# The first two value projections of a decoder block as seven block products, and the convolution's layer norm by token halves

## The chip, the cores and the metric

The kernel runs on one core of a Trainium2 chip. A core has a matrix engine (PE, whose weight loads the profile lists apart as PEld), a vector engine (DVE), a scalar engine (ACT), a general engine (POOL) and a queue that issues transfers (SP). Each engine runs its own instructions in a fixed order, and semaphores hold an instruction until what it needs is there. The metric is the device time of one execution in microseconds; the kernel before takes 1676.24 us in the median of three runs (1675.69 to 1677.17).

## The reference

One layer of a decoder block for 1024 tokens of 1024 channels, all float32. What matters here:

```
h  = rms_norm(x)
z  = h @ w_in            # q, k, v (3 groups x 8 heads x 64 each), conv input, two gates
o_g = attention of head group g on q, k, v     (g = 0, 1, 2; dilations 1, 4, 16)
u  = causal depthwise conv (31 taps) of a gated linear unit of z
m  = mean over the 1024 channels of u, per token
u  = silu((u - m) * rsqrt(mean((u - m)^2) + 1e-5) * g + b)     # layer norm, then swish
y  = u @ w_conv_out + b_conv_out
x  = x + rms_norm((sigmoid(z_ga) * y_attn + sigmoid(z_gc) * y) @ w_mix_out)
x  = x + rms_norm(swiglu_ffn(rms_norm(x)))
```

The value projection is `v = h @ w_v`, 1024 x 1024 times 1024 x 1536. The kernel cuts its columns into six jobs of 256: head group g (0, 1, 2) by half hg of its heads (0, 1).

## The kernel before, in words

**Number format.** Every float32 product is made of three products of rounded parts: a matrix is split into `hi` (a copy rounded to the matrix engine's format, by ACT) and `lo` (what is left, a subtraction by DVE or POOL), and hi*hi, hi*lo and lo*hi are added up in PSUM.

**Stages.** The convolution's inputs, the gates, and the 12 query and key pairs (`qk_pair`) come first. Each of these takes two jobs at once by `winograd`: the two jobs' weights by two halves of the contraction make a 2 x 2 block matrix A, the tokens by halves another one B, and seven block products of sums of blocks (A11, A12, A22, S1 to S4 with B11, B21, B22, T1 to T4) take the place of eight. The token operands, sums of halves already split, lie in SBUF as `B.T`. Then come the six value jobs, each by `v`, with the plain eight block products; then one gate, the convolution's output projection, the attention's, the mix and the FFN.

**What sets the order.** It is written out by hand. `tick()` is called after every few matmuls; it runs the steps that were put down for that tick (`later(n, step)`, in n ticks), splits one piece of the next weights every PIECE ticks, and moves every generator in `B.gens` on by one step; a generator that yields n rests n ticks. `beat()` is called more often and moves one generator, `B.fine`, at a rate: this is the attention, whose matmuls are so strewn between those of the value jobs. A tile that is taken from a pool of fixed size waits until the last reader of the tile that lay there is done.

**The value jobs** (`v`, L1114 to L1165). A job takes 8 token tiles by 8 contraction tiles. For each, one matmul (L1139) multiplies the tokens' hi by a weight tile that holds hi and lo side by side (512 columns), and one (L1140) the tokens' lo by hi (256 columns). ACT copies the 512 columns out (L1150), and POOL adds the two halves (L1161). The weights' split is L207 (ACT) and L208 (DVE). A tick falls after every two such pairs, 32 ticks a job.

**The convolution's norm** (`conv_norm`, L1488 to L1540) is a generator that runs beside the value jobs. It loads the eight channel blocks (128 channels by 1024 tokens), gets the mean by a product of the blocks' sum with a constant column (L1503; the sum is finished by a POOL addition, L893), subtracts it (DVE, L1512), squares (ACT, L1515), adds the squares up (DVE, L1518), and calls `rstd`: eight products of one column each (L469), a square root on ACT (L473), small steps on DVE, and eight transposes (L484) that spread the result over the partitions. Then it multiplies (DVE, L1530) and applies the swish (ACT, L1533). ACT changes its function table where the kind of function changes (ACT_TABLE_LOAD at L473, L1533 and L1538).

**The attention** (`attention`) starts when the norm's generator has ended (`normed` is 9). `double` (POOL, L1078 to L1080) lays out the keys of a head pair for two halves of the sequence: one operand z for each half, one part for each head. The scores are L1262 and L1266, the exponentials L1280, the transposes L1305 and the products with the values L1339.

## Time and profile before

| | |
|---|---|
| median of three runs | 1676.24 us |
| the profiled execution's own time | 1676.75 us |
| its span, first to last instruction | 1675.0 us |
| PE busy | 1658.9 us, 99% of the span |
| DVE, ACT, POOL busy | 1272.3, 828.3, 542.5 us |
| granted PE clock | 0.999 |
| value jobs' matmuls L1139 and L1140 | 384 of each, first at 544.2 us, last at 769.2 us |
| first attention matmul L1262 | 608.5 us |

A row of the timeline gives start, duration, engine, line, operation, tiles, partitions or columns of the weights, shape, and how many instructions were merged; brackets at its end hold the idle time before it and what ended that. A matmul's duration runs from its start until its result has drained, and matmuls overlap, so what one costs is the step from its start to the next one's. A row of a group gives its busy time, the mean of one in ns, and the idle time before it with what ended that.

### The profile page before, as it was taken

The page shows a single profiled execution, that of the slowest core. Times are in us where ns is not written, and L with a number is a line of the kernel's source. Part 1 is how long each engine was busy: PE and PEld are TensorE (multiplying, and loading weights), DVE is VectorE, ACT ScalarE, POOL GpSimd, SP SyncE. Part 2 cuts the span into 40 slices and gives each one's busy share as a digit, 9 for nine tenths or more (in the row PEclk, how much of TensorE's full clock was granted, in tenths as well). Part 3 has the DMA queues.
Part 4 walks back from the last instruction along what each step waited for, and adds up shares of the span by engine and source line. Part 5 has one row for each costly group of instructions (what it writes and reads, how often), then busy time and mean ns, then how long its engine had stood idle before and what let it go on. Part 6 is the DMA issues. An engine that isn't in the chain of part 4 may idle for free.

```text
span 1675.0 us, 23388 instructions
## 1 busy us (share of the span) xinstructions
PE 1658.9 (99%) x8027; PEld 1384.6 (83%) x8027; DVE 1272.3 (76%) x2268; ACT 828.3 (49%) x1646; POOL 542.5 (32%) x456
## 2 busy tenths in 40 slices
PE   9999999999999999999999999999999999999998
PEld 7787888888888889988788888888888888888886
DVE  7998987789899768778876746877655566576686
ACT  7454443443444588888713357633333333354453
POOL 0038777787876366877300300000000000000000
PEclk9999999999999999999999999999999999999999
DMA  4435433455566987879998524134232223494334
GB/s 182 153 102 187 143 132 126 153 176 192 177 176 161 286 273 224 257 220 286 297 272 310 176 88 171 56 132 151 84 118 94 95 95 119 165 375 120 115 119 157
DMA packets 165178, 289.64 MB, mean 173 GB/s; under 512 B 47689, under 2 KB 79812, under 8 KB 165060
## 3 DMA queue, kind: packets, MB, share of 16 engines
q1 hardware_dynamic: 164420, 287.45, 52.5%
q8 instruction: 63, 1.03, 0.3%
q14 instruction: 55, 0.45, 0.1%
q10 hardware_dynamic: 288, 0.52, 0.1%
q0 software_dynamic: 352, 0.18, 0.1%
HBM read 197.39 MB, written 95.42 MB: 175 GB/s over the span
## 4 chain that ended last, share of the span: by engine, by line
PE 87%; issue 5%; DVE 2%; POOL 2%; ACT 2%; DMA 1%; SPq 0%; DVEq 0%; ACTq 0%; POOLq 0%
PE p L354 16%; PE p L353 16%; PE p L352 16%; PE p L2282 13%; PE p L2026 5%; PE p L1139 5%; PE p L336 2%; PE p L337 2%; PE p L338 2%; PE p L1140 2%; PE p L655 2%; PE p L1339 2%; PE p L1305 1%; PE p L1266 1%; PE p L1262 1%
## 5 line engine op out<-in xcount | busy, mean ns | idle before, releaser
L352 PE MATMUL p<-b,b 128*128 128x512 f32 x1316 | 512.7, 390 | 0.1
L354 PE MATMUL p<-b,b 128*128 128x512 f32 x1316 | 512.4, 389 | 0.2
L353 PE MATMUL p<-b,b 128*128 128x512 f32 x1316 | 512.2, 389 | 0.1
L352 PEld LDWEIGHTS p<-b,b 128*128 128x128 f32 x1316 | 247.1, 188 | 52.7 <-ACT c L411 0.5
L354 PEld LDWEIGHTS p<-b,b 128*128 128x128 f32 x1316 | 247.1, 188 | 52.5 <-POOL b L215 1.5
L353 PEld LDWEIGHTS p<-b,b 128*128 128x128 f32 x1316 | 247.1, 188 | 51.7 <-DVE b L1477 0.5
L2282 PE MATMUL p<-b,b 128*128 128x512 f32 x924 | 209.6, 389 | 0.0
L2282 PEld LDWEIGHTS p<-b,b 128*128 128x128 f32 x924 | 173.5, 188 | 36.0
L868 DVE SCALAR_TENSOR_TENSOR p<-b,par,p 128x511 f32<-128x511 f32 (+14 forms) x232 | 163.6, 738 | 0.0
L1139 PE MATMUL p<-b,b 128*128 128x512 f32 x384 | 144.2, 408 | 0.1
L214 ACT CAST b<-d 128x1024 fp32r<-128x1024 f32 x82 | 86.1, 1050 | 100.7 <-POOL d L237 56.6
L215 POOL TENSOR_TENSOR b<-d,b 128x1024 fp32r<-128x1024 f32 x43 | 104.2, 2422 | 47.6 <-ACT b L214 39.0
L1477 DVE TENSOR_TENSOR b<-b,b 128x512 fp32r<-128x512 f32 x141 | 98.9, 708 | 16.0 <-ACT b L1476 14.4
L215 DVE TENSOR_TENSOR b<-d,b 128x1024 fp32r<-128x1024 f32 x39 | 47.6, 1221 | 79.3 <-ACT b L214 79.3
L1140 PE MATMUL p<-b,b 128*128 128x256 f32 x384 | 107.7, 280 | 0.0
L1476 ACT CAST b<-b 128x512 fp32r<-128x512 f32 x141 | 86.4, 619 | 40.9 <-PE p L2282 18.5
L336 PE MATMUL p<-b,b 128*128 128x512 f32 x240 | 96.3, 401 | 0.0
L214 ACT CAST b<-b 128x1024 fp32r<-128x1024 f32 x51 | 53.6, 1052 | 85.0 <-POOL b L246 38.7
L1280 ACT ACTIVATE c<-c,stat 128x128 f32<-128x128 f32 (+1 forms) x192 | 85.2, 447 | 18.2 <-DVE stat L1270 16.9
L337 PE MATMUL p<-b,b 128*128 128x512 f32 x240 | 93.6, 390 | 0.0
L338 PE MATMUL p<-b,b 128*128 128x512 f32 x240 | 93.6, 390 | 0.0
L2026 PE MATMUL p<-b,b 128*128 128x512 f32 x384 | 89.9, 392 | 0.0
(248 smaller groups left out, 2897.0 us busy)
## 6 DMA issues: line engine op xcount, KB each, us to landing
b<-w_in SPq DMA_DIRECT2D x33, 512.0 KB, 5.8
b<-w_fi SPq DMA_DIRECT2D x29, 512.0 KB, 4.4
d<-w_in SPq DMA_DIRECT2D x25, 512.0 KB, 4.2
dk<-c SPq DMA_DIRECT2D x48, 256.0 KB, 4.3
dq<-c SPq DMA_DIRECT2D x48, 256.0 KB, 3.6
b<-dk SPq DMA_DIRECT2D x48, 256.0 KB, 6.2
d<-w_fi SPq DMA_DIRECT2D x22, 512.0 KB, 3.5
dqS<-c SPq DMA_DIRECT2D x44, 256.0 KB, 2.1
```

What stands on the lines that cost most here:

```text
L214: self.nc.scalar.copy(hi, x)
L215: self.wsplit.tensor_tensor(lo, x, f(hi), op=OP.subtract)
L336: nc.tensor.matmul(ps, hi[:, s], a, start=kt == 0, stop=False)
L337: nc.tensor.matmul(ps, hi[:, s], b, start=False, stop=False)
L352: nc.tensor.matmul(ps, hi[:, s], a, start=first and kt == 0, stop=False, skip_group_check=True)
L353: nc.tensor.matmul(ps, hi[:, s], b, start=False, stop=False, skip_group_check=True)
L354: nc.tensor.matmul(ps, lo[:, s], a, start=False, stop=kt == 3, skip_group_check=True)
L868: nc.vector.scalar_tensor_tensor(A[i][:, j:], src[i][:, :H - j], w[i], A[i][:, j:], op0=OP.mult, op1=OP.add)
L1139: nc.tensor.matmul(ps, a, w, start=kt == 0, stop=kt == KT - 1, skip_group_check=True)
L1140: nc.tensor.matmul(ps[:, 256:], b, w[:, :256], start=False, stop=kt == KT - 1, skip_group_check=True)
L2026: nc.tensor.matmul(banks[tt][nh], st, wt[:, nh * H:(nh + 1) * H], start=bool(kt == 0 and a), stop=bool(kt == KT - 1 and b))
L2282: nc.tensor.matmul(acc[t], x, y, start=first and e == 0, stop=last and e == 2, skip_group_check=True)
```

## The change

Two of the six value jobs, (g, hg) = (0, 0) and (1, 0), are done together by a new function `quad` in the block form that the query and key pairs use, with seven products of 48 matmuls of 256 columns each. Here the tokens are the stationary side and the weights the moving side. The other four keep `v`. `quad` has its own loads, sums (DVE) and splits (cast on ACT, subtraction on POOL), written by ticks. Results leave PSUM by ACT copies and DVE additions.

`conv_norm` works by halves of the tokens (512 each): it takes its blocks half by half, and calls `rstd` twice, for 512 tokens each. The eight small products of the first half are issued while the squares of the second half run, those of the second half while the first half is multiplied and passed through the swish. It starts with the block products rather than with the first value job. The attention's first step (loads) and the laying out of all four parts of its first keys (`double`) are now put down by ticks before the first scores; the second half's parts were laid out at the head pair's second score step before.

```diff
+    def quad_split(self, q, name):
...
+        hi, lo = self.slot(F32R), self.slot(F32R)
+        nc.scalar.copy(hi, x)
...
+        nc.gpsimd.tensor_tensor(lo, x, f(hi), op=OP.subtract)
+        q["w"][name] = hi, lo
...
+    def quad_prod(self, ps, w, rhs, first):
+        nc = self.nc
+        hi, lo = w
+        for kt in range(4):
+            a, b = rhs[kt]
+            n = slice(kt * 256, (kt + 1) * 256)
+            for c in range(4):
+                o = ps[c // 2][:, c % 2 * 256:(c % 2 + 1) * 256]
+                t = slice(c * 128, (c + 1) * 128)
+                nc.tensor.matmul(o, a[:, t], hi[:, n], start=first and kt == 0 and c % 2 == 0, stop=False,
+                                 skip_group_check=True)
+                nc.tensor.matmul(o, a[:, t], lo[:, n], start=False, stop=False, skip_group_check=True)
+                nc.tensor.matmul(o, b[:, t], hi[:, n], start=False, stop=kt == 3 and c % 2 == 1, skip_group_check=True)
+                if c % 2:
+                    self.tick()
+
+    def quad(self, q, T, then):
...
+        ja, jb = q["jobs"]
+        for k, step in ((1, lambda: self.quad_split(q, "A12")), (5, lambda: self.quad_sum(q, "S4")),
+                        (9, lambda: self.quad_split(q, "S2")),
+                        (17, lambda: self.quad_split(q, "S1")), (25, lambda: self.quad_split(q, "S3")),
+                        (33, lambda: self.quad_split(q, "S4")), (41, lambda: self.quad_split(q, "A22"))):
+            self.later(k, step)
...
+        X, Z = two(), two()
+        self.quad_prod(X, w.pop("A11"), operands("B11"), True)
+        x1 = copy(X, ja, True)
+        self.quad_prod(Z, w.pop("A12"), operands("B21"), True)
+        add(Z, x1, ja, 0)
+        Z = x1 = None
+        self.quad_prod(X, w.pop("S2"), operands("T2"), False)
+        x2 = copy(X, ja)
+        V = two()
+        self.quad_prod(V, w.pop("S1"), operands("T1"), True)
+        v1 = copy(V, jb)
+        self.quad_prod(X, w.pop("S3"), operands("T3"), False)
+        add(X, v1, jb, 1)
+        v1 = None
+        self.quad_prod(V, w.pop("S4"), operands("B22"), False)
+        add(V, x2, ja, 1)
+        V = x2 = None
+        self.quad_prod(X, w.pop("A22"), operands("T4"), False)
+        o = result()
+        for b in range(2):
+            nc.scalar.activation(ordered(o[b], jb[0][0]), plain(X[b]), AF.Identity, scale=-1.0)
...
@@ attention @@
-        self.later(17, lambda p=nxt: self.double(p, 0))
+        for i in range(4):
+            self.later(17 + 2 * i, lambda p=nxt, i=i: self.double(p, i // 2, (i % 2,)))
...
-                if u == 1:
-                    self.double(cur, 1, (1,) if cur[2]["z"][1] else (0, 1))
+                if u == 1 and s:
+                    self.double(cur, 1, (1,))
...
@@ conv_norm @@
+        for j in range(4):
+            self.later((1, 3, 8, 11)[j], lambda j=j: load(0, j))
+        yield 5
+        means = [average(0), average(1)]
...
+        def total(hf):
+            scale[hf] = self.rstd(q[hf][0], H, self.eps_ln, 0)
+            next(scale[hf])
+            q[hf] = None
...
         for hf in range(2):
...
+            mean, means[hf] = means[hf], None
+            for b in range(10):
+                if b < 8:
+                    add(A[hf, b], A[hf, b], mean, op=OP.subtract)
+                if 0 < b < 9:
+                    q[hf].append(self.half())
+                    nc.scalar.activation(q[hf][-1], A[hf, b - 1], AF.Square)
...
+                if hf and b == 4:
+                    total(0)
+                if hf == 0 and b > 5:
+                    load(1, b - 6)
+                yield 1
+            mean = None
+        for hf in range(2):
+            rs = scaled(hf)
+            for b in range(9):
+                if hf == 0 and b == 4:
+                    total(1)
+                if b < 8:
+                    add(A[hf, b], A[hf, b], rs, op=OP.mult)
+                if b:
+                    a = A.pop((hf, b - 1))
+                    nc.scalar.activation(a, a, AF.Silu, bias=self.col(C_BLN + b - 1), scale=self.col(C_GLN + b - 1))
...
+                yield b % 2
...
@@ build @@
+    vs = list(vj.values()) + [late[:1] or co[:1]]
+    for i, q in enumerate(B.quads):
+        if i == QUADS - 1:
+            B.later(33, lambda: B.load_ahead(vs[0][0]))
+            B.later(43, lambda: next(att))
+            B.later(36, lambda: B.load_ahead(vs[0][1]))
+            B.later(41, lambda: B.queue_split(vs[0][1]))
+        B.quad(q, B.T, B.quads[i + 1] if i + 1 < QUADS else None)
+    B.T = None
+    B.banks(g=2, s=2, t=2, o=2)
```

In the rows below a matmul's names are its result, then its moving and its stationary operand. Line numbers of the kernel before are its own; in the changed kernel `quad_prod` is L1218 to L1221, the value jobs' pair is L1144 and L1145, L469 has become L474, and L207 has become L209.

**PE, where the value stage starts.** First the kernel before:

```order
L354 MATMUL p_4710<-b_1092,b_4770 128x512
L1139 MATMUL p_4880<-b_4800,b_631 128x512
L1140 MATMUL p_4880<-b_4800,b_631 128x256
L1139 MATMUL p_4880<-b_4800,b_642 128x512
L1140 MATMUL p_4880<-b_4800,b_642 128x256
L1139 MATMUL p_4880<-b_4820,b_652 128x512
L1140 MATMUL p_4880<-b_4820,b_652 128x256
```

and the changed one:

```order
L358 MATMUL p_4710<-b_1092,b_4774 128x512
L1218 MATMUL p_4872<-b_4818,b_631 128x256
L1220 MATMUL p_4872<-b_4819,b_631 128x256
L1221 MATMUL p_4872<-b_4818,b_631 128x256
L1218 MATMUL p_4872<-b_4818,b_631 128x256
L1220 MATMUL p_4872<-b_4819,b_631 128x256
L1221 MATMUL p_4872<-b_4818,b_631 128x256
L1218 MATMUL p_4873<-b_4818,b_631 128x256
```

The pair of 512 and 256 columns has given way to three matmuls of 256 columns, and the weights' hi and lo (`b_4818`, `b_4819`) are tiles of their own.

**PE, where the seventh block product ends and the first value job begins** in the changed kernel:

```order
L1221 MATMUL p_4872<-b_5271,b_1092 128x256
L474 MATMUL p_5421<-mean_col,c_5330 128x1 x4
L1218 MATMUL p_4873<-b_5271,b_1092 128x256
L1220 MATMUL p_4873<-b_5272,b_1092 128x256
L1221 MATMUL p_4873<-b_5271,b_1092 128x256
L1218 MATMUL p_4873<-b_5271,b_1092 128x256
L1220 MATMUL p_4873<-b_5272,b_1092 128x256
L1221 MATMUL p_4873<-b_5271,b_1092 128x256
L1144 MATMUL p_5457<-b_5321,b_631 128x512
L1145 MATMUL p_5457<-b_5321,b_631 128x256
```

The small products of the norm's second half (L474) stand six matmuls ahead of the first value job; its transposes follow 12 pairs into that job, and the first half's transposes stand six matmuls into the seventh product. The first scores of the attention follow 46 pairs into that job; before, they followed 168 pairs into the value stage.

**ACT, around the same place** in the changed kernel:

```order
L1677 COPY c_5368<-p_5363 128x512
L1707 ACT_TABLE_LOAD
L1707 ACTIVATE b_4896<-b_4896,par 128x512
L209 CAST b_5395<-b_5216 128x2x256
L1707 ACTIVATE b_4896<-b_4896,par 128x512
L1707 ACTIVATE b_4911<-b_4911,par 128x512
L478 ACT_TABLE_LOAD
L478 ACTIVATE st_5426<-p_5421,eps_ln 128x4
L1707 ACT_TABLE_LOAD
L1707 ACTIVATE b_4911<-b_4911,par 128x512
L209 CAST b_5443<-b_5216 128x2x256
L1707 ACTIVATE b_4966<-b_4966,par 128x512
```

L1677 copies out the first half's transposes, L1707 is the swish, L478 the square root, and the two L209 rows are the third and the last quarter of the first value job's weights. Behind the last row stand the two copies that empty the PSUM tiles of the seventh product (L1308). The kernel before has one table load for the square root and one for the swish, and two quarters of a later job's weights between the swish's instructions.

**POOL, from the end of the block products to the attention's values** in the changed kernel:

```order
L1199 TENSOR_TENSOR b_5272<-d_4738,b_5271 128x1024
L1083 MEMSET b_5486 64x512
L1084 CAST b_5486<-b_5294 64x512
L1085 CAST b_5300<-b_5292 64x512
L1083 MEMSET b_5486 64x512
L1084 CAST b_5486<-b_5297 64x512
L1085 CAST b_5302<-b_5292 64x512
L1083 MEMSET b_5529 64x512
L1084 CAST b_5529<-b_5294 64x512
L1085 CAST b_5300<-b_5292 64x512
L1166 TENSOR_TENSOR d_5534<-b_5456 128x512
L1083 MEMSET b_5529 64x512
```

`b_5486` and `b_5529` are the attention's first key operands for the two halves (L1083 to L1085 are L1078 to L1080 of the kernel before). Those of the second half now stand around the addition for the first job's first two token tiles (L1166); before, they stood behind ten such additions, in the third job, and were issued at the second step of the scores.

186 lines of the change are left out of this document (128 added, 58 removed).

## The prediction

> **What bounds the kernel now.** I read the page first, then the groups by line and form, then PE's timeline where the change sits, and last who waited for whom there.
>
> ```profile
> span 1675.0 us, 23388 instructions
> ...
> PE 1658.9 (99%) x8027; PEld 1384.6 (83%) x8027; DVE 1272.3 (76%) x2268; ACT 828.3 (49%) x1646; POOL 542.5 (32%) x456
> ...
> PE 87%; issue 5%; DVE 2%; POOL 2%; ACT 2%; DMA 1%; SPq 0%; DVEq 0%; ACTq 0%; POOLq 0%
> ```
>
> PE is busy 99% of the span and carries 87% of the chain of waits. So only two things move the time: matmul work that goes away, and gaps on PE that go or come. The other engines count where PE waits for them. The profiled execution took 1676.75 us, 0.5 above the median of 1676.24; the sum is made against it and the 0.5 taken off at the end.
>
> What a matmul costs is the step to the next one's start:
>
> ```profile
> 544.93 0.28 PE L1140 MATMUL p<-b,b 128*128 128x256 f32 x1
> ...
> 547.75 0.28 PE L1140 MATMUL p<-b,b 128*128 128x256 f32 x1
> ...
> 644.45 0.40 PE L1266 MATMUL p<-b,b 128*128 128x256 f32 x2
> 644.68 0.40 PE L1139 MATMUL p<-b,b 128*128 128x512 f32 x1
> ...
> 639.64 0.40 PE L1266 MATMUL p<-b,b 128*128 128x256 f32 x2
> 639.88 0.60 PE L1305 MATMUL p<-ident,c 128*128 128x128 f32 x4
> ```
>
> Between the first two rows lie eight pairs of 512 and 256 columns: 2.82 us, 0.353 a pair. Two matmuls of 256 columns back to back, with different weights, take 0.23 us (644.45 to 644.68) to 0.24 us (639.64 to 639.88): 0.115 to 0.12 each.
>
> Three gaps of the value stage lie in the change's reach, its start, the mean's products, and the first scores:
>
> ```profile
> 543.75 0.39 PE L354 MATMUL p<-b,b 128*128 128x512 f32 x1
> 544.24 0.50 PE L1139 MATMUL p<-b,b 128*128 128x512 f32 x1
> 544.57 0.28 PE L1140 MATMUL p<-b,b 128*128 128x256 f32 x1
> ...
> 548.29 1.98 PE L1503 MATMUL p<-b,mean_col 128*128 128x512 f32 x4 [0.26 <-POOL b L893]
> 549.71 0.79 PE L1139 MATMUL p<-b,b 128*128 128x512 f32 x1
> 550.34 0.28 PE L1140 MATMUL p<-b,b 128*128 128x256 f32 x1
> ...
> 611.38 0.31 PE L1262 MATMUL p<-b,b 128*128 128x256 f32 x1
> 612.96 0.39 PE L1262 MATMUL p<-b,b 128*128 128x256 f32 x1 [1.27 <-POOL b L1079]
> 613.18 0.28 PE L1266 MATMUL p<-b,b 128*128 128x256 f32 x1
> 613.63 0.39 PE L1266 MATMUL p<-b,b 128*128 128x256 f32 x1 [0.17 <-POOL b L1080]
> 613.85 0.39 PE L1139 MATMUL p<-b,b 128*128 128x512 f32 x1
> ```
>
> At the start PE loses 0.26 us (0.49 for a step of 0.23) and 0.10 behind it (0.33 for 0.23). The mean's products come 0.42 us late (548.29 minus 547.75 minus 0.12). At the first scores the four steps from 611.38 to 613.85 take 2.47 us where four matmuls of 256 columns take 0.47: 2.0 us, waiting for POOL's layout of the second half's keys.
>
> **The change, part by part.**
>
> *Matmuls.* Away go two of six jobs, 2 x 64 = 128 pairs: 128 x 0.353 = 45.2 us. In come 7 x 48 = 336 matmuls of 256 columns: at 0.117, 39.3 us. That is 5.9 less; by the bounds 0.115 and 0.12 it is 6.6 to 4.9 less.
>
> Each of these matmuls loads weights of its own, and the trace shows where the load runs:
>
> ```profile
> 545.29 0.28 PE L1140 MATMUL p<-b,b 128*128 128x256 f32 x1
> 545.29 0.19 PEld L1139 LDWEIGHTS p<-b,b 128*128 128x128 f32 x1
> 545.40 0.40 PE L1139 MATMUL p<-b,b 128*128 128x512 f32 x1
> ```
>
> The load starts with the matmul of 256 columns ahead of it and does not move the next one, which starts 0.11 later. The Trainium skill ("TensorE: Matmul & The Clock Gate", section "Measured speedup vs the span model") has the rule that a load overlaps a running matmul only if it goes to another group of rows; by it every load here, all 128 rows wide, would stand exposed. The trace disagrees; what such a price would give is the last rival.
>
> *The norm's small products.* Their number is the same, split in two:
>
> ```profile
> 579.24 1.68 PE p L469 x16
> ...
> 585.89 0.87 PE p L484 x8
> ```
>
> The 1.68 and 0.87 us move from the value jobs to the block products and the first job. No idle time stands before them here, so issuing them later removes none. Each switch from and to them costs about 0.1, and there are two more places: +0.2.
>
> *Start.* The first block product needs A11's split. That is put down 19 ticks into the last key pair (28 ticks of three matmuls, some 19 us), so it is cast and subtracted by about 541.7 (538.1 plus 1.05 plus 2.41, rows below), 2.5 us ahead, and its PSUM tiles wait for no DVE addition. The 0.36 goes. Bounds 0 and 0.36; I take -0.4 with rounding.
>
> *The mean.* POOL's last addition waits for DVE (L881), which now has S1's sum ahead of it (1024 elements for a split of 512, about 0.5 later), so it ends near 548.75, not 548.2. PE comes to the mean after 42 matmuls, 544.0 + 4.9 = 548.9: just late enough. The 0.42 shrinks by 0.3 (bounds: 0.2 worse, 0.4 better). Behind this addition stands A12's subtraction on POOL, done at 548.75 + 2.41 = 551.2; the second product starts at 551.7 (48 x 0.117 and the mean's four of 0.43).
>
> *Splits of the later products.* Each is put down eight ticks, one product or 5.6 us, ahead.
>
> ```profile
> L214 ACT CAST b<-d 128x1024 fp32r<-128x1024 f32 x82 | 86.1, 1050 | 100.7 <-POOL d L237 56.6 <-DVE d L237 43.3 <-POOL b L256 0.7
> L1150 ACT COPY b<-p 128x512 f32<-128x512 f32 x48 | 28.0, 583 | 14.3 <-PE p L1140 12.8 <-POOL d L1161 1.4
> L215 POOL TENSOR_TENSOR b<-d,b 128x1024 fp32r<-128x1024 f32 x43 | 104.2, 2422 | 47.6 <-ACT b L214 39.0 <-issue 6.5 <-POOL b L256 1.5
> 507.48 2.78 POOL L215 TENSOR_TENSOR b<-d,b 128x1024 fp32r<-128x1024 f32 x1
> ```
>
> Ahead of it on ACT lie two copies out of PSUM (2 x 0.58), then the cast (1.05) and POOL's subtraction (2.42, at worst 2.78): 4.6 to 5.0 of 5.6 us. So PE waits for none, at a margin of 0.6 to 1.0 us. It is thin, and the cover is ACT being free: the squares of the norm share its queue.
>
> *End of the block products.* Here I expect a new wait. From the first half's transposes on, six matmuls into the seventh product, ACT has in its queue: copy, table load, swish, cast, two swishes, table load, square root, table load, swish, and the cast of the first value job's last quarter; DVE's subtraction follows.
>
> ```profile
> 586.36 1.08 ACT L1526 COPY b<-p 128x512 f32<-128x512 f32 x2 [0.49 <-PE p L484]
> 587.46 1.28 ACT L1533 ACT_TABLE_LOAD   x1
> 588.75 1.24 ACT L1533 ACTIVATE b<-b,par 128x1024 f32<-128x1024 f32 x1
> ...
> 580.96 0.27 ACT L473 ACTIVATE st<-p,eps_ln 128x8 f32<-128x8 f32 x1 [1.15 <-PE p L469]
> L958 ACT ACTIVATE c<-c 128x512 f32<-128x512 f32 x14 | 8.8, 631 | 0.0
> L207 ACT CAST b<-b 128x512 fp32r<-128x512 f32 x24 | 14.8, 615 | 0.4 <-DMA b<-w_v 0.3
> 582.33 0.69 DVE L208 TENSOR_TENSOR b<-b,b 128x512 fp32r<-128x512 f32 x1
> ```
>
> With 0.63 for a swish of 512 elements (the sigmoid's row, L958), that is 0.58 + 3 x 1.28 + 4 x 0.63 + 0.27 + 2 x 0.62 + 0.69 = 9.1 us. PE gets there in 36 x 0.117 + 0.84 (half of 1.68) + 6 x 0.117 + 6 x 0.353 = 7.9 us. It waits 1.3. The second token tile takes the PSUM tile of the seventh product, which ACT empties behind one more swish with two copies: 8.45 + 0.63 + 2 x 0.58 = 10.2 against PE's 9.1 + 0.7 = 9.8, another 0.4. Together +1.7. Bounds: 0, if ACT overlaps its instructions' ends (by 0.1 each in the rows above, one us in all) and runs ahead; 3.5, if DVE's small steps of the norm hold the swishes up. The square root stands on PE's own small products, so ACT cannot run far ahead.
>
> In the rows above the copies end at 587.44, the load runs from 587.46, and the swish starts at 588.75: a switch costs its row of 1.28 here and nothing beside it. The Trainium skill ("ScalarE: Activation LUTs", section "What ACT_TABLE_LOAD costs") adds a drain of 1.38 us to each load. By that page the three loads would take 4.1 us more (an estimate); the trace does not show it at this one switch.
>
> *First scores.* All four parts of the first keys are laid out some 14 pairs before the first score. The 2.0 us goes unless another engine is late there; next in line are the exponentials on ACT, which the swish has used until shortly before, and POOL's value parts, which have less ahead of them now. I take -2.0 (bounds 0 and -2.0).
>
> *Unchanged.* The attention still finds about as many pairs to hide in (210 after its start, before 384 - 168 = 216).
>
> Sum: -5.9 - 0.4 - 0.3 - 2.0 + 0.2 + 1.7 = -6.7; 1676.75 - 6.7 = 1670.05, less 0.5: **1669.6 us**.
>
> **Rivals.**
>
> *The table loads stay hidden* (ACT is ahead, first value job starts clean): 1669.6 - 1.7 = 1667.9. For it: ACT is only 49% busy. Against: the order puts the square root, which needs PE's products, ahead of the cast.
>
> *The first scores wait again*, for exponentials or values: 1669.6 + 2.0 = 1671.6. For it: ACT's queue is fuller than before. Against: ten us pass between the chain above and the scores.
>
> *Splits come late* (slower): each of six splits behind A11's needs cast, then POOL, while the norm's squares, which wait for DVE and its loads, stand ahead of the cast on ACT. DVE's subtractions stretch beside POOL's work, too (0.69 above, 1.37 here):
>
> ```profile
> 583.18 1.29 POOL L1161 TENSOR_TENSOR d<-b 128x512 f32<-128x512 f32 x1 [6.13 <-ACT b L1150]
> 583.65 1.37 DVE L208 TENSOR_TENSOR b<-b,b 128x512 fp32r<-128x512 f32 x1 [0.64 <-ACT b L207]
> ```
>
> If each came 1.6 us late, 6 x 1.6 = 9.6 us would be lost: 1669.6 + 9.6 = 1679.2. It decides from 1.1 us a split on, where the 6.7 is used up; each would have to take 1.7 to 2.1 us more than the sum above.
>
> *A table switch costs ACT twice its row* where it stands between busy instructions: 3 x 1.28 = 3.8 more on the chain above, all of it waited for, 1669.6 + 3.8 = 1673.4. The switch at 587.46 speaks against it, three in a row are not in this trace. This is the place of the drain that the page on ScalarE has.
>
> *Loads stand exposed*: with the 0.19 us of the PEld row added to each of 336 matmuls, 64 us: about 1733. The 0.23 us for two speaks against it.
>
> *The change does not do what it says* in one respect under every case: the small products waited for nothing before.
>
> **How the numbers follow.** Forecast 0.50; loads hidden 0.15; scores wait 0.16; splits late 0.09; dear table switches 0.04; exposed loads 0.01; 0.05 for shifted gaps in the later attention, either way by up to 4 us. A measurement of this kernel tells about 0.2% (3.4 us) from no change, so faster means under 1672.9. The forecast, hidden loads and the scores' wait lie there, less some of their tails: 0.82. The dear switches and the tails give 0.11 for the same; late splits and exposed loads mostly slower: 0.07. The range takes in the bounds of the matmul's price (-0.7 to +1.0) and of the new wait (-1.7 to +1.8), and reaches to the scores' wait and the dear switches: 1666.0 to 1674.5.
>
> **What would show it.** Steps between quad_prod's starts of 0.115 to 0.12, and 41 to 44 us from its first matmul to its last with the small products in. No idle time before the first product, the mean, and the first L1413 rows with POOL. A wait of 1 to 3 us on PE at L1144, twelve matmuls into the first value job, with ACT or DVE as releaser and three table loads in a row on ACT. Late splits would show as waits of L1220 for POOL. The forecast is wrong if those add up to over 3 us, or if the gaps behind 614 us grow as much as the block products save.

## The result, and the profile after

| | before | after |
|---|---|---|
| median, six runs of each on one chip | 1676.21 us | 1687.59 us |
| lowest and highest | 1675.69, 1677.17 | 1685.01, 1689.56 |
| profiled execution, its span | 1676.75, 1675.0 | 1687.49, 1685.7 |
| ratio after to before, 95% interval | | 1.0066, 1.0053 to 1.0079 |

The change costs 11.4 us where 6.6 less were forecast. PE is as busy as before, and only 1.4 us of its busy time are gone, where 4.9 to 6.6 us of matmul were to go:

```profile
span 1685.7 us, 23624 instructions
...
PE 1657.5 (98%) x8107; PEld 1388.9 (82%) x8107; DVE 1286.5 (76%) x2298; ACT 831.9 (49%) x1656; POOL 551.3 (33%) x455
```

**The block products cost what was said.** PE's timeline after the change, from the last matmul of the key pairs to the mean's products, and a later piece:

```profile
543.64 0.39 PE L358 MATMUL p<-b,b 128*128 128x512 f32 x1
543.87 0.28 PE L1218 MATMUL p<-b,b 128*128 128x256 f32 x1
...
548.90 1.88 PE L1653 MATMUL p<-b,mean_col 128*128 128x512 f32 x4
...
568.90 0.28 PE L1218 MATMUL p<-b,b 128*128 128x256 f32 x1
570.19 0.39 PE L1220 MATMUL p<-b,b 128*128 128x256 f32 x1 [1.01 <-POOL b L1199]
```

The first starts a step of 0.23 behind the pairs. From 543.87 to 548.90 lie 42 steps, 0.120 each, and the mean's products follow without a wait. So three terms of the sum hold, the price of a matmul (at the dear end of its bounds), the start and the mean. The last row is a split that came late.

**Where PE waits.** The view of waits, PE after the change, 540 to 900 us; columns are the time waited in all, how often, and the longest:

```profile
PE p L1144 <- DVE b L210: 6.7, 2, 5.8
PE p L1490 <- ACT c L1463: 4.3, 2, 2.8
...
PE p L1220 <- POOL b L1199: 1.0, 1, 1.0
```

The first row is the forecast's new wait at the first value job, and it is 6.7 us, not 1.7. PE's rows around it:

```profile
593.58 0.28 PE L1145 MATMUL p<-b,b 128*128 128x256 f32 x1
599.70 0.80 PE L1144 MATMUL p<-b,b 128*128 128x512 f32 x1 [5.84 <-DVE b L210]
600.29 0.42 PE L1145 MATMUL p<-b,b 128*128 128x256 f32 x1
...
600.93 0.42 PE L1145 MATMUL p<-b,b 128*128 128x256 f32 x1
```

Behind the wait the pair of matmuls takes 0.64 us (600.29 to 600.93), where it took 0.353. The windows view says why. Its columns are the busy time of PE, PEld, DVE, ACT and POOL with the number of instructions, then the granted clock, the share of the DMA engines and GB/s:

```profile
594.60:598.02 3.42, 0.00 (x0) 0.00 (x0) 1.48 (x6) 3.36 (x5) 0.94 (x2) 1.00 0.20 77
598.02:601.43 3.41, 1.73 (x5) 1.54 (x6) 2.49 (x5) 3.41 (x7) 0.00 (x0) 0.50 0.31 107
601.43:604.84 3.41, 3.41 (x13) 3.02 (x13) 0.02 (x1) 1.80 (x4) 0.00 (x0) 0.50 0.90 257
604.84:608.26 3.42, 3.42 (x21) 2.96 (x21) 2.84 (x5) 2.66 (x5) 0.68 (x1) 1.00 0.84 230
```

The granted clock falls to a half while PE stands still, and stays there until 604.84, five microseconds after the work has come back.

**What made it late.** DVE and ACT after the change, on their own timelines. On DVE:

```profile
568.19 2.49 DVE L1690 TENSOR_TENSOR c<-c,c 128x512 f32<-128x512 f32 x1 [0.55 <-ACT c L1687]
...
577.45 0.68 DVE L1690 TENSOR_TENSOR c<-c,c 128x512 f32<-128x512 f32 x1
579.67 2.90 DVE L1690 TENSOR_TENSOR c<-c,c 128x512 f32<-128x512 f32 x1
```

On POOL at the same time:

```profile
567.76 2.38 POOL L1199 TENSOR_TENSOR b<-d,b 128x1024 fp32r<-128x1024 f32 x1 [5.66 <-ACT b L1196]
...
579.21 2.81 POOL L1199 TENSOR_TENSOR b<-d,b 128x1024 fp32r<-128x1024 f32 x1 [2.83 <-DVE rs L483]
```

The same addition takes 0.68 us alone and 2.5 to 2.9 beside POOL's subtraction; it ends 0.55 us after POOL does, a little less than its own time (568.19 + 2.49 = 570.68, POOL 567.76 + 2.38 = 570.14; 582.57 and 582.02). Over the block products, DVE was busy 42.9 us in 45.4; in the same stretch before the change it was 32.8. The windows rows, first of after, then of before:

```profile
545.00:590.40 45.40, 43.77 (x352) 42.24 (x352) 42.92 (x50) 23.85 (x37) 20.40 (x10) 1.00 0.76 223
```

```profile
545.00:590.40 45.40, 45.14 (x260) 38.56 (x259) 32.80 (x31) 25.58 (x37) 15.67 (x13) 1.00 0.87 273
```

DVE is the third pair of columns: 42.92 and 32.80. Its groups by line and form, 544 to 591 us after and 545 to 590.4 us before, are for the norm's subtractions and its sum of squares:

```profile
L1690 DVE TENSOR_TENSOR c<-c,c 128x512 f32<-128x512 f32 x14 | 15.4, 1098 | 2.1 <-ACT c L1687 1.9
L1684 DVE TENSOR_TENSOR b<-b,c 128x512 f32<-128x512 f32 x16 | 14.3, 921 | 0.0
```

```profile
L1512 DVE TENSOR_TENSOR b<-b,b 128x1024 f32<-128x1024 f32 x8 | 11.8, 1491 | 3.9 <-ACT b L1504 3.9
L1518 DVE TENSOR_TENSOR b<-b,b 128x1024 f32<-128x1024 f32 x7 | 11.6, 1664 | 0.2
```

The same work takes 29.7 us instead of 23.4, and beside it stand the block products' sums (four rows, 8.0 us) and additions out of PSUM (six rows, 3.9 us). Those six have an operand in PSUM, and their groups have means of 0.67 to 0.68. So DVE has little slack, what passes it in order comes late, and ACT, whose order mixes casts, swishes and square roots, waits for it with the first value job's casts in its queue:

```profile
586.65 0.58 ACT L1677 COPY c<-p 128x512 f32<-128x512 f32 x1
587.24 1.28 ACT L1707 ACT_TABLE_LOAD   x1
590.63 0.82 ACT L1707 ACTIVATE b<-b,par 128x512 f32<-128x512 f32 x1 [2.11 <-DVE b L1704]
591.36 0.60 ACT L209 CAST b<-b 128x512 fp32r<-128x512 f32 x1
...
593.90 0.81 ACT L1707 ACTIVATE b<-b,par 128x512 f32<-128x512 f32 x1 [1.23 <-DVE b L1704]
594.73 1.28 ACT L478 ACT_TABLE_LOAD   x1
596.02 0.26 ACT L478 ACTIVATE st<-p,eps_ln 128x4 f32<-128x4 f32 x1
596.30 1.28 ACT L1707 ACT_TABLE_LOAD   x1
597.60 0.81 ACT L1707 ACTIVATE b<-b,par 128x512 f32<-128x512 f32 x1
598.32 0.60 ACT L209 CAST b<-b 128x512 fp32r<-128x512 f32 x1
```

L209 at 598.32 is the cast of the last quarter; DVE's subtraction behind it (598.95, 0.69 us) ends at 599.64, and PE goes on at 599.70. How much of this is DVE's fullness and how much ACT's order, the experiments tell: in e3 DVE is just as full, and the wait is gone.

**The account.** For each pair of matmuls that follow each other, a step is the time from start to start; its loss is the step less what the fastest quarter of such steps (same two lines of code, same sizes) takes in all the kernels run here. Summed over the trace, by stage:

| | before | after | difference |
|---|---|---|---|
| steps without loss | 1626.5 | 1622.2 | -4.3 |
| loss up to the value stage | 5.8 | 5.7 | -0.1 |
| start and mean | 1.4 | 0.6 | -0.8 |
| block products, or the first 39 us of value jobs | 0.6 | 2.2 | +1.7 |
| from there to the first score | 0.3 | 9.9 | +9.6 |
| the first scores (6 us) | 2.5 | 0.9 | -1.6 |
| attention beside value jobs | 13.2 | 13.4 | +0.1 |
| attention behind the value jobs | 11.6 | 15.8 | +4.2 |
| the rest, FFN included | 4.4 | 6.2 | +1.8 |

(Where fewer than 40 such steps exist, the fastest is taken. The size of a step is that of the moving operand; where the columns of the stationary one are told apart too, the 4.2 becomes 3.3.) The differences sum to +10.6, the time by which the two traces differ from first to last matmul. Of the 9.6, 7.05 are the two waits and 2.4 the half clock; of the 4.2, 1.5 is the half clock again (816.47 to 819.88 us). The 1.8 at the end is one wait:

```profile
1468.78 0.96 PE L2467 MATMUL p<-b,b 128*128 128x512 f32 x3 [1.51 <-DVE c L2354]
```

The first output of the FFN goes into a PSUM bank that the stage ahead of it still reads. Before the change PE waits for nothing there. That the output then went into another bank, and that the order in which the banks came free had changed with the attention, is the likely reason, but no view here shows the banks.

### The profile page after: what moved, and what is told of

The parts are those of the page before. It is cut to its first block, busy times and chain, and to the rows that moved or that the text cites. A ratio compares the mean times of both kernels' runs of the same rounds, so it can differ in the third digit from the quotient of the medians.

```text
span 1685.7 us, 23624 instructions
## 1 busy us (share of the span) xinstructions
PE 1657.5 (98%) x8107; PEld 1388.9 (82%) x8107; DVE 1286.5 (76%) x2298; ACT 831.9 (49%) x1656; POOL 551.3 (33%) x455
## 4 chain that ended last, share of the span: by engine, by line
PE 58%; DVE 3%; ACT 2%; DMA 2%; issue 1%; POOL 0%; DVEq 0%; SPq 0%; POOLq 0%; ACTq 0%
PE p L2467 12%; PE p L357 8%; PE p L358 8%; PE p L356 8%; PE p L2211 5%; PE p L1144 3%; PE p L340 3%; PE p L341 2%; PE p L342 2%; PE p L1490 2%; PE p L1456 1%; PE p L1145 1%; PE p L1417 1%; PE p L1413 1%; DMA dact<-b 1%
## 5 line engine op out<-in xcount | busy, mean ns | idle before, releaser
L356 PE MATMUL p<-b,b 128*128 128x512 f32 x1316 | 512.7, 390 | 0.0
L358 PE MATMUL p<-b,b 128*128 128x512 f32 x1316 | 512.4, 389 | 0.2
L357 PE MATMUL p<-b,b 128*128 128x512 f32 x1316 | 512.2, 389 | 0.1
L2467 PE MATMUL p<-b,b 128*128 128x512 f32 x924 | 209.7, 389 | 1.5 <-DVE c L2354 1.5
L1628 DVE TENSOR_TENSOR b<-b,b 128x512 fp32r<-128x512 f32 x141 | 99.4, 711 | 15.9 <-ACT b L1627 14.2
L1144 PE MATMUL p<-b,b 128*128 128x512 f32 x256 | 100.2, 417 | 6.7 <-DVE b L210 6.7
L340 PE MATMUL p<-b,b 128*128 128x512 f32 x240 | 96.8, 403 | 0.0
L341 PE MATMUL p<-b,b 128*128 128x512 f32 x240 | 94.0, 392 | 0.0
L342 PE MATMUL p<-b,b 128*128 128x512 f32 x240 | 93.9, 391 | 0.0
L2211 PE MATMUL p<-b,b 128*128 128x512 f32 x384 | 90.0, 392 | 0.0
L217 POOL TENSOR_TENSOR b<-b,b 128x1024 fp32r<-128x1024 f32 x24 | 57.7, 2405 | 86.6 <-ACT b L216 86.6
```

What stands on the lines that cost most here:

```text
L217: self.wsplit.tensor_tensor(lo, x, f(hi), op=OP.subtract)
L340: nc.tensor.matmul(ps, hi[:, s], a, start=kt == 0, stop=False)
L341: nc.tensor.matmul(ps, hi[:, s], b, start=False, stop=False)
L342: nc.tensor.matmul(ps, lo[:, s], a, start=False, stop=kt == nk - 1)
L356: nc.tensor.matmul(ps, hi[:, s], a, start=first and kt == 0, stop=False, skip_group_check=True)
L357: nc.tensor.matmul(ps, hi[:, s], b, start=False, stop=False, skip_group_check=True)
```

## The experiments

Each run is compared with runs of the kernel before on the same chip; the ratio is to that, with its 95% interval. The runs were made on more than one chip (e1 to e4, e5 to e8 and e9 to e12 each on one), so a difference of times between two groups is the looser one. Three theories are told apart. A: the block products are worth their steps, and what eats them is the norm that shares ACT and DVE with them (A1: by ACT's order; A2: because DVE is full, so that a wait only moves; A3: the square root and the swishes hold whatever stands behind them). B: the norm by halves is itself the loss. C, in the expectations of e1, e2 and e10: block products are dear as such.

**e1, the norm and the keys without block products.** The kernel before takes the changed kernel's `conv_norm` whole, and the early layout of the keys:

```diff
-        self.later(17, lambda p=nxt: self.double(p, 0))
+        for i in range(4):
+            self.later(17 + 2 * i, lambda p=nxt, i=i: self.double(p, i // 2, (i % 2,)))
```

> The norm by token halves and the early layout of the first keys, beside six plain value jobs (no block products). Theory A (the block products leave ACT and DVE too little time for the norm; each part alone is harmless): the start of the value jobs loses no more than before, the mean and the first scores' 2.0 us go, so 1673.5 to 1676 us, against 1676.2 for the kernel before. Rival B (the norm by halves itself, its two more table loads and its second chain of small products, makes the wait): the 6 us wait for the fourth weight quarter is there too, 1680 or more. Rival C (the block products as such are dearer than their steps): as A here, and the other runs with block products stay over 1684.

Measured: 1678.19 us, 1.0011 (1.0001 to 1.0020). There is no wait of 6 us, so B falls; but the gain that A names is not there either. PE's three longest waits from 543 to 640 us:

```profile
PE p L1340 <- ACT c L1313: 1.3, 1, 1.3
PE p L1267 <- DMA b<-dq: 0.9, 1, 0.9
PE p L1139 <- DVE b L208: 0.9, 1, 0.9
...
```

The waits for POOL have gone, and as much has come at other places: a weight quarter 0.9 late, queries whose load has not landed, a cast of probabilities.

**e2, block products with the norm of before.**

The changed kernel takes back the whole `conv_norm` of the kernel before; beside the block products it gets its PSUM tiles where they get theirs:

```diff
-            ps = self.bank("s")
+            ps = self.bank("s" if "s" in self.tags else "g")
```

> Block products as in the changed kernel, but the norm of the kernel before beside them (whole blocks of 1024 tokens, one chain of small products). Theory A: block products need their splits on time from ACT and POOL, and the whole-block squares stand ahead of the casts on ACT, so the late splits return in greater number: waits of the block products for POOL of 5 to 12 us in all, and 1679 to 1690. Rival B (the norm by halves is what makes the wait): no wait of more than 1 us in the block products or the first value job, 1669 to 1673. Rival C: over 1684, without a wait that the trace shows.

Measured: 1693.18 us, 1.0098 (1.0083 to 1.0113). This is theory A, and more than the 1679 to 1690 that it said. PE's longest wait, 543 to 640 us:

```profile
PE p L1220 <- POOL b L1199: 10.4, 3, 6.9
...
```

Three splits come late, one by 6.9 us. So the norm by halves is not what hurts; beside the norm of before, with its own pauses, the block products cost some 5.6 us more.

**e3, both square roots together.** The changed kernel with the second half's small products and root ahead of all swishes:

```diff
+        yield 5
+        total(1)
+        yield 1
         for hf in range(2):
             rs = scaled(hf)
             for b in range(9):
-                if hf == 0 and b == 4:
-                    total(1)
```

> The changed kernel with one edit: the second half's small products and square root come five ticks after its squares, ahead of all swishes, so that ACT has one table load for both square roots and one for the swishes, and the first value job's four weight casts and the last copy out of the block products stand ahead of the swishes in ACT's queue. Theory A1 (the order of ACT's queue makes the 6 us wait): the waits of 1.0 and 6.0 us at the first value job go, with them the granted clock of 0.60 behind them (2.9 us), and the attention starts some 5 us earlier: 1674 to 1678, and 1671 if the later attention's 5.7 us hang on its late start. Rival A2 (DVE is full, 43.5 of 46 us, so the wait moves elsewhere): at least 5 us of new waits of PE for DVE between 575 and 610 us, 1682 or more.

Measured: 1678.95 us, 1.0010 (1.0000 to 1.0019), 8.6 less than the changed kernel. That is just above the 1674 to 1678 of A1. The profiled execution, at 1681.61 us, is the longest of the ten. PE's waits, 543 to 640 us:

```profile
PE p L1413 <- DVE stat L1421: 1.8, 1, 1.8
PE p L1220 <- POOL b L1199: 1.0, 1, 1.0
...
PE p L1144 <- DVE b L210: 0.2, 1, 0.2
```

6.7 us have become 0.2, with the amount of work on ACT less by two table loads and on DVE the same:

```profile
545.00:590.40 45.40, 43.76 (x349) 42.11 (x347) 42.92 (x49) 23.51 (x36) 18.99 (x7) 1.00 0.79 231
```

DVE is busy 42.92 us of 45.40, to the hundredth as in the changed kernel. So a full DVE alone does not make PE wait at the first value job; with the changed kernel's order on ACT it does. This supports A1, though the edit does not tell the order from the two table loads that it saves. A2 expected 5 us of new waits; they are not there, but 1.8 us of waiting came at the first scores (L1413). Of the 8.6 us, 1.8 are the wait at the FFN's first output, which is not in this trace and has nothing to do with the theory.

**e4, POOL's subtraction replaced by copies.** The kernel leaves out the remainder of the block products' weights.

```diff
-        nc.gpsimd.tensor_tensor(lo, x, f(hi), op=OP.subtract)
+        nc.gpsimd.tensor_copy(lo, f(hi))
+        nc.gpsimd.tensor_copy(lo, f(hi))
```

> The changed kernel, with the block products' remainder (lo) not computed: POOL writes two plain copies of hi into lo in place of the subtraction, about as long (2 x 1.1 us for 2.4), but with one input from SBUF. This leaves out part of the computation. Theory P (a two-input addition of DVE, both inputs in SBUF, is held for the whole of a two-input POOL operation, and that is what makes DVE late): the norm's additions and subtractions on DVE (4 to 7 rows of 2.3 to 3.2 us) are back to 0.68 us, the late split of the fifth product goes, the 6.0 us wait shrinks to 0 to 3 us; 1676 to 1682. Rival (DVE's time is the table loads' and ACT's): DVE's rows get shorter but the wait stays over 5 us, 1685 or more.

Measured: 1682.28 us, 1.0033 (1.0021 to 1.0045), just above the range of theory P. The late split of the fifth product went, but one of 0.7 us came in the second; the wait shrank from 6.7 to 4.7 us, not to 3 or less; and DVE's rows did not go back to 0.68:

```profile
568.54 1.09 DVE L1691 TENSOR_TENSOR c<-c,c 128x512 f32<-128x512 f32 x1 [0.55 <-ACT c L1688]
...
578.88 1.52 DVE L1691 TENSOR_TENSOR c<-c,c 128x512 f32<-128x512 f32 x1
```

Beside these POOL was copying (568.04 to 569.08 and 578.40 to 579.86). So "with two inputs on POOL" was wrong: a copy with one input holds DVE as well, only for a shorter time, since each copy is shorter. Over 545 to 590.4 us DVE was busy 42.6 us, 0.3 less than in the changed kernel, so the run does not tell what part of the wait comes from POOL's hold on DVE. The Trainium skill ("SBUF — State Buffer", section "Who interferes with whom") has it so: a DVE instruction with two inputs in SBUF contends with any instruction of POOL that reads SBUF. The rows here agree.

**e5, the first value job's casts earlier.**

```diff
-            B.later(33, lambda: B.load_ahead(vs[0][0]))
+            B.later(17, lambda: B.load_ahead(vs[0][0]))
...
-            B.later(36, lambda: B.load_ahead(vs[0][1]))
-            B.later(41, lambda: B.queue_split(vs[0][1]))
+            B.later(20, lambda: B.load_ahead(vs[0][1]))
+            B.later(25, lambda: B.queue_split(vs[0][1]))
```

> The changed kernel with one edit: the first value job's weights are loaded and split 16 ticks earlier, in the middle of the block products; the two square roots stay where the change has them. Theory A1 in its simple form (the casts only stand in the wrong place of ACT's queue): the waits of 1.0 and 6.0 us at the first value job go and nothing comes for them, 1676 to 1679. Theory A3 (what holds ACT is the second half's square root with its two table loads and the swishes, which wait for the sums and transposes; whatever stands behind them is late, and DVE, 43.5 of 46 us busy, has no room for the four subtractions ahead of them): the wait moves, to the block products (2 to 3 us, for DVE) and to the last copy out of the block products, which stands behind the same swishes (3 to 4 us at the first value job): 1683 to 1688.

Measured: 1686.05 us, 1.0065 (1.0051 to 1.0078). PE's waits, 543 to 640 us:

```profile
PE p L1144 <- ACT b L1308: 2.9, 1, 2.9
PE p L1218 <- DVE b L1274: 2.2, 1, 2.2
```

As A3 said, the wait moves: to the last copy out of the block products, which stands behind the same swishes, and to a DVE addition. Moving the casts, which only stand behind what waits, gives nothing that can be told from the changed kernel (1.0065 against its 1.0066); moving the square root took the ratio down to 1.0010.

**e6, e3 with four splits put down one or two ticks earlier.**

```diff
-                        (17, lambda: self.quad_split(q, "S1")), (25, lambda: self.quad_split(q, "S3")),
-                        (33, lambda: self.quad_split(q, "S4")), (41, lambda: self.quad_split(q, "A22"))):
+                        (16, lambda: self.quad_split(q, "S1")), (23, lambda: self.quad_split(q, "S3")),
+                        (32, lambda: self.quad_split(q, "S4")), (40, lambda: self.quad_split(q, "A22"))):
```

> The kernel with the square roots together (e3), and four splits put down one or two ticks earlier (16, 23, 32, 40 in place of 17, 25, 33, 41). Theory S (a split is late because it was put down a block product's length ahead, with 0.6 us to spare by the sum, and DVE's late rows eat more than that): the wait of 1.17 us of the fifth product goes, 1.0 to 1.5 us less than e3: 1677.5. Rival (POOL is late because DVE holds its input back, wherever the step is put): the wait stays, 1679.

Measured: 1677.03 us, 1.0005 (0.9996 to 1.0014). The wait of L1220 for POOL is gone from the view of waits, as theory S said. The median is 1.9 us under that of e3, where 1.0 to 1.5 were said, but on another chip, and the intervals of the two ratios overlap; so the trace shows that the wait went, and the time does not show what that was worth.

**e7, e6 without the exponential that ends the norm.**

```diff
-            if hf:
-                nc.scalar.activation(rs[:, :1], self.eps_ln, AF.Exp)
```

> As e6, and without the one-element exponential that ends the norm and brings ACT's table load for the attention ahead of it; the load comes with the first real exponential. In e3 a cast of the next weights stands behind that load (1.28 us), DVE's subtraction behind the cast, and the first scores' reduction behind that: PE waits 1.9 us at the first scores, and the window of 3.4 us around it is less than half busy, so the next one runs at half clock. Theory E: the wait shrinks to under 1 us, the clock stays at 1.00, 2 to 3 us less than e6: 1674.5 to 1675.5. Rival (the first exponential then comes late and the transposes wait for it): no gain, 1677.5.

Measured: 1675.80 us, 0.9997 (0.9989 to 1.0006): no different from the kernel before, and 11.8 less than the changed one, of which 1.8 are again the FFN's. The wait at L1413 fell from 2.0 us in e6 to 0.4. The gain over e6 is 1.2, not 2 to 3. In e6's trace the clock had not fallen there: PE was busy 1.87 us of the clock's window around that wait (613.48 to 616.89), more than half of it.

**e8, e3 with the attention moved on faster.**

```diff
-RV, RU = 0.42, 0.8
+RV, RU = 0.46, 0.8
```

> The kernel with the square roots together (e3), and the attention moved on at 0.46 steps a beat in the value jobs instead of 0.42. In e3 194 value pairs are left when the attention starts (216 before, 210 in the changed kernel), and 157 products with the values are left when the value jobs end (120 and 127); what PE loses behind the value jobs is 14.9 us (10.7 and 15.1). Theory C (the attention is worth its time only beside value pairs; fewer pairs leave more of it to a stage where each product waits): 120 or fewer left at 0.46, loss behind the value jobs 11 us or less, loss within them up by 1 to 2 us; with the first output of the FFN waiting 1.7 us again (its accumulator lies in the bank that the stage ahead uses last, as in the changed kernel), 1677 to 1680. Rival (the loss behind the value jobs has another cause, such as the half clock): it stays at 14 to 15 us, 1681 or more.

Measured: 1684.17 us, 1.0046 (1.0030 to 1.0061). Theory C of this run falls. Left when the value jobs end were 124 products instead of 157, near the 120 that it said, but the loss behind them was 16.4 us (1.5 of it half clock), not 11, and the loss beside them rose from 13.0 to 15.9. The FFN's 1.8 us are in this trace and not in that of e3.

**e9 and e10, without the norm's arithmetic.** The norm is replaced, in the kernel before (e9) and in the changed one (e10), by loads and stores: `move(j)` loads block j of the convolution and, eight ticks later, stores it as the norm's result. The 84 is 76 in e10; both then have 210 value pairs left at the first score.

```diff
+        for j in range(8):
+            move(j)
+            yield 4
+        yield 84 - 44
+        self.normed = 9
```

> The kernel before with the norm's arithmetic left out: its blocks are only loaded and stored again, and the attention is let go at a fixed tick, so that 210 value pairs are left at the first score. This leaves out part of the computation. It is the base for the next run, which differs from it in the block products alone. The mean's and the norm's small products (about 6 us of PE) are not there: 1668 to 1672, no wait between 545 us and the first score, and the attention loses what it does in the other kernels, 25 to 27 us in all.

> The changed kernel with the same norm left out in the same way, and the attention let go with the same 210 value pairs left. Theory A (the block products are worth their steps, and what eats them is the norm that shares ACT, DVE and POOL with them): no late split, no wait at the first value job, and 4 to 6 us less than the run with plain value jobs. Rival D (the block products make the later attention lose some 3 us more by themselves, as the kernels with them lose 13.5 to 15.5 us behind the value jobs and those without 10.3 to 11.6): only 1 to 3 us less. Rival C (block products dear as such): no less, or more.

Measured: e9 1674.67 us (1673.22 to 1675.66), 0.9988 (0.9979 to 0.9998), where 1668 to 1672 were expected; e10 1673.65 us (1672.04 to 1679.03), 0.9990 (0.9981 to 0.9999). The two cannot be told apart (the means of their ten runs each are 1674.64 and 1674.63), where theory A expected 4 to 6 us less for e10. In time that is what rival C said. e10's profiled run, at 1675.93 us, is one of its longer ones. Its longest wait from 543 to 640 us, and two windows of it:

```profile
PE p L1220 <- POOL b L1199: 1.7, 1, 1.7
...
```

```profile
548.99:552.40 3.41, 1.68 (x15) 1.47 (x14) 3.31 (x2) 1.17 (x2) 2.77 (x1) 1.00 0.96 192
552.41:555.82 3.41, 3.41 (x19) 3.41 (x18) 1.65 (x2) 1.05 (x1) 1.76 (x1) 0.50 0.99 383
```

There is no wait at the first value job: that part of A holds. Nor are the products dear as such: the steps without loss take 4.6 us less in e10's trace than in e9's. But about 5.5 us more are lost: 2.3 ahead of the first score, 0.9 at the first scores, 1.3 beside the value jobs and 1.2 behind them. The second product's split is late by 1.7 us, because the mean's products, which in the changed kernel give POOL 1.7 us of cover, are not there; and the half-empty window costs the next one half its clock (1.5 us). Behind the value jobs the run with block products lost 15.5 us and the plain one 14.3, of each about 1.5 half clock. So rival D's 3 us are not shown: between before (216 pairs, 11.6) and e9 (210 pairs, 12.9 without the clock) lies as much as between e9 and e10 (13.9), and the last difference shrinks to 0.4 where steps are told apart by the columns of the stationary operand too.

**e11, the kernel before with the keys laid out early, and nothing else** (the diff of e1 without the norm).

> The kernel before with one part of the change alone: all four parts of the first keys are laid out ahead of the first scores. The prediction's term was 2.0 us for the first scores. Theory: the waits of PE for POOL at the first scores go (1.3 and 0.2 us by the chain of waits, 1.8 by the steps), another wait of up to 0.8 us for DVE takes their place: 1675.0 to 1675.6. Rival (the exponentials or a table load are next in line and hold PE as long): 1676.2, no change.

Measured: 1675.58 us, 1.0004 (0.9994 to 1.0015). The waits of 1.3 and 0.2 us for POOL are gone, one for DVE is there:

```profile
PE p L1263 <- DVE stat L1271: 0.7, 2, 0.5
```

The loss at the first scores fell from 2.5 to 1.5 us. The term of 2.0 us was worth 1.0 on its own, too little to be told from no change. Four of the eleven runs took 1679.69 to 1681.25 us, at a mean granted clock of 0.997 or 0.998 where the others had 0.999; the trace is of a fast one and does not show what they waited for.

**e12, e11 without the last exponential and with the norm's closing pause cut.**

```diff
-        nc.scalar.activation(rs[:, :1], self.eps_ln, AF.Exp)
         rs = None
-        yield 11
+        yield 5
```

> The kernel before with the keys laid out early, without the one-element exponential at the norm's end (as e7), and with the pause behind it cut from 11 ticks to 5, so that the attention starts some 4 us earlier beside 12 more value pairs. Theory: no wait at the first scores and less left of the attention behind the value jobs: 1673 to 1675, under both kernels. Rival (the first exponential's table load comes late, and the attention's waits only move): 1676.

Measured: 1676.65 us, 1.0009 (1.0000 to 1.0018). This is the rival: PE now waits 1.6 us for queries that are still on their way from memory (L1267, DMA b<-dq) and 1.0 for a cast of probabilities.

No kernel of the twelve that computes everything beats the kernel before; e6, e7 and e11 cannot be told from it.

## Why the prediction was wrong, step by step

*Matmuls: right, at the edge of their bounds.* 336 steps of 0.120 are 40.3 us, 4.9 less than the 45.2 taken out: the upper bound of the price, not the 0.117 taken. From first to last the block products took 46.6 us (543.87 to 590.44), not 41 to 44: to the 40.3 come 4.0 of small products and 2.2 of loss. The steps came as said; but the kernel did not get shorter by them, and e9 and e10 show that here it doesn't even without the norm's arithmetic.

*Start and mean: right.* -0.7 were said for both, and -0.8 came: of the old 1.4 of loss 0.6 are there now, half of them at the second product's split (A12). POOL took 3.34 us for it where 2.41 were counted, and it had been left 0.5.

*First scores: right in kind, near in size.* -2.0 was said, -1.6 came (in e11, alone, -1.0).

*Splits of the later products: wrong by a little.* "PE waits for none, at a margin of 0.6 to 1.0 us." One did: 1.17 us, the fifth. The sum counted ACT's and POOL's own rows and took the cast as soon as it was put down. e6, on top of e3, removes it with two ticks, so the rule of one product ahead was too short. Another 0.7 us went to an addition of DVE that was late (L1274, at 583.31), which the sum had not looked at.

*End of the block products: the step that failed.* The mechanism was named (three table loads, swishes and a square root ahead of the last cast), the place was right (twelve matmuls into the first value job, with DVE as releaser), and the price was 1.7 with a bound of 3.5 where 7.05 came. The chain was 9.1 us in the sum. From the transposes (584.09) to the end of DVE's subtraction (599.64) it took 15.55. PE's and ACT's rows at its start:

```profile
584.09 0.60 PE L489 MATMUL p<-ident,rs 128*128 128x128 f32 x4
...
584.40 0.63 ACT L1687 ACTIVATE c<-b 128x512 f32<-128x512 f32 x1 [3.97 <-DVE b L1684]
```

- 2.5 us: ACT does not begin with the copy. Two squares of the second half and two casts of weights stand ahead of it, late because DVE's subtraction of the mean was (3.97 us of idle time in this row); the copy starts at 586.65.
- 3.3 us: the swishes wait for DVE's products, 2.11 and 1.23 in the rows above.
- 0.7 us: a swish takes 0.81, not the sigmoid's 0.63, four times.

Together 9.1 + 6.5 = 15.6. PE needed 8.6 us rather than 7.9, and 15.6 - 8.6 = 7.0 is what it waited. So the sum added up ACT's work and left out that ACT waits. The bound of 3.5 was meant for "if DVE's small steps of the norm hold the swishes up", but no budget of DVE was made for the stage. The rows of before gave 32.8 us of work there; the block products' four sums (1024 elements, some 1.2 each where nothing stretches them) and six additions (0.68) add 9 to 12, which makes 42 to 45 in 46 us. The stretching was quoted among the rivals (1.37 for 0.69) and applied to the splits, not to the norm's rows. From the sum's -6.7 to the traces' +10.6 are 17.3 us: 7.9 of them lie in this step, with the half clock behind it, 4.2 behind the value jobs, 1.8 in the FFN, 1.7 inside the block products, 1.4 in the matmuls and small products, and 0.3 elsewhere. So this is the largest miss, and not the only one.

*The clock: not in the sum at all.* Every wait was priced at its own length. The 7.05 us cost 2.4 more at half clock, and a wait of 2.8 us in the later attention 1.5 more. The Trainium skill ("TensorE: Matmul & The Clock Gate", section "What's actually happening") states the gate and its window of 3413 ns; the kernel before shows no window at half clock between its first microseconds and its end, and I priced the waits as if none could come.

*Unchanged attention: wrong.* "Still finds about as many pairs to hide in" (210 for 216): it loses 4.2 us more behind the value jobs. 1.5 is the clock. A plain kernel with 210 pairs loses 1.3 more than before without the clock (e9), and the block products about 1 more than that (e10). Why they do stays open; e8 shows that driving the attention faster is not the remedy. The prediction's own sign, gaps behind 614 us that grow as much as the block products save, came: 0.1, 4.2 and 1.8 us more, against 4.9 saved.

*The FFN's 1.8 us* belong to no step. They are in the traces of the changed kernel, e4, e5, e8, e9 and e10, and not in those of the kernel before, e1, e2, e3, e6, e7, e11 and e12, all with the same FFN. The block products can't be the reason, since e9 has none. Whether a kernel has them is taken as luck here, good or bad.

*Rivals.* "Loads stand exposed" fell with the steps of 0.120 us. The rule that the prediction quotes for it from the Trainium skill ("TensorE: Matmul & The Clock Gate") stands there in the section "The mechanism", and the same section lets a load run ahead into a background weight buffer, so the page as a whole does not ask for exposed loads. "Splits come late" had the right side and 1679; its path was not the one. In e2 it is the path. The table switch at twice its row fell again: in the rows above the load at 594.73 ends where the square root starts (596.02), and the next at 596.30 ends where the swish starts. The Trainium skill's drain of 1.38 us a load ("ScalarE: Activation LUTs", section "What ACT_TABLE_LOAD costs") is not in these rows.

## What to carry to other kernels

When a stage is made shorter on the engine that bounds it, divide the work of each other engine in that stage by the new length before believing the gain: here DVE went from 72% to 95%. That alone is a warning and no loss (e3 is as full and does not wait there); the loss came where a queue that mixes late work with urgent work, ACT's, handed the lateness on to PE. In an in-order queue move the instruction that waits (here the square root with its two table loads), not the ones that stand behind it. A wait of PE of more than half a clock window (half of 3.41 us) may cost up to 1.7 us more, an estimate from the windows below. And compare two kernels that differ in the gaining part alone (here e9 and e10): a gain in the steps can be gone from the total.

## What had not been expected of the hardware

The granted clock goes by windows of 3.413 us that run freely through the execution: all changes of the clock in a trace lie whole multiples of that apart (598.02 and 816.47 us here: 64 of them). In the 14 traces of this case, outside the start and the end of the program, 14 windows at full clock in which PE was busy 0.48 of the time or less were each followed by one at half clock; of six between 0.49 and 0.54 three were; of those of 0.55 and more none. A window at half clock with PE busy throughout costs 1.7 us at most, half its length (an estimate; 1.5 us were lost from 816.47 to 819.88). The page of the Trainium skill named above says that the clock falls after an idle window; here half an idle one is enough, and a wait of 1.8 us is, when it falls into one window (e3):

```profile
614.87:618.28 3.41, 1.64 (x11) 1.33 (x11) 1.84 (x9) 2.81 (x9) 3.25 (x4) 1.00 1.03 320
618.28:621.70 3.42, 3.42 (x14) 3.12 (x14) 1.72 (x11) 2.54 (x11) 0.80 (x1) 0.50 1.06 323
```

Where the windows lie differs between executions: in the 14 traces their grid starts anywhere from 0.1 to 3.2 us behind the first instruction. So nearly the same wait at the same place had a half-clock window behind it in e3 (1.8 us) and none in e6 (2.0 us, PE busy 0.55 of its window). This is probably part of why some kernels spread so far: e10 took 1672.04 us at a mean granted clock of 0.999 and 1679.03 at 0.996. But 0.003 of 1676 us are 5 of these 7 us, so the rest has another cause that stays open.
